# One VectorE operation for mask, negation, copy and row minimum in the attention of a hybrid decoder kernel

## The chip, the cores and the metric

The kernel runs on one core of one Trainium2 chip. Its engines work side by side and are tied by semaphores: TensorE (PE) for matmuls, with its weight loads (PEld), VectorE (DVE), ScalarE (ACT), GpSimd (POOL) and SyncE (SP), which here only issues transfers. The metric is the device time of one execution in microseconds (us), the median of several runs.

## The reference

Everything is float32, with 1024 positions of width 1024. One RG-LRU layer comes first, then one attention layer of 8 heads, whose keys and values are projected from the stream after the first layer, and a last norm. The attention works on blocks of 128 queries, and a causal mask leaves a query the keys up to its own place:

```
def one_block(args):                     # one block of 128 queries
    qn_b, qr_b, bi = args
    s = einsum("bqhd,bkhd->bhqk", qn_b, k_nope) + einsum("bqhr,bkr->bhqk", qr_b, k_rope)
    s = s * ATTN_SCALE
    mask = kpos[None, :] <= (bi * 128 + arange(128))[:, None]
    p = softmax(where(mask, s, -inf), axis=-1)
    return einsum("bhqk,bkhd->bqhd", p, v)
...
o = lax.map(one_block, ...)              # 8 blocks x 8 heads
y = o * silu(gate);  x = x + y @ w_out;  return rms_norm(x, final_norm)
```

## The kernel before

Each float32 operand of a matmul is split in a high half and a low half, and a product is the sum of three matmuls. The high half is an ACT copy (L82), the low half a DVE subtraction that follows it (L83).

The attention runs from about 528 to 785 us, some 31 us a head. For each head `kq` projects keys and queries (matmuls at L114 to L116), `vals` the values of two heads (L839 to L841). Query block number qb sees nk = 128(qb+1) keys, so the eight blocks of a head have 128, 256, ... 1024 columns. In the text a block goes by its columns ("block 1024"). `scores` does, for one block:

- five matmuls on each stretch of up to 512 columns (L857 to L861) into a tile `s` of PSUM, of which there are two;
- L862, DVE: the triangular 128x128 mask is added to the last 128 columns, in PSUM;
- L864, DVE: the negated maximum of each row, over the whole block, into `m`;
- L867, ACT: exp(s + m) from PSUM into a page of SBUF, with the row sum `l`; a second instruction reads the sum out (ACTIVATION_READ_ACCUMULATOR in the trace). Its end gives the tile `s` back;
- L868 and L869, DVE: one over `l`, and the page times it.

Then `transposes` turns the page by TensorE in squares of 128 (L877) into PSUM tiles `pm`, and L82 and L83 split them into `pt`. After every fourth block `pv` multiplies values by `pt` (L892 to L894), and L896 multiplies by the gate. Scores are issued two blocks ahead (LOOK = 2).

In the last head the output projection is prepared too: `wout` loads a slice of its weights (L920 by SP into `wr`, of which there are two; L922 by POOL) and makes its low half on DVE (L923), and `dpart` runs first parts of that projection on TensorE while blocks are waited for. 36 pages of 128x1024 in SBUF are shared by all of this.

The order of the instructions on each engine is fixed at build time by a scheduler that follows priorities. At run time each engine goes through its list in order and waits where an operand or a buffer is not ready.

Of the kernel before, what the change touches and what calls it, by code (L numbers as in the profile page):

```python
# [9 lines left out]
F32 = mybir.dt.float32  # L10
F32R = mybir.dt.float32r
AF = mybir.ActivationFunctionType
ALU = mybir.AluOpType
AX = mybir.AxisListType
# [3 lines left out]
S = 1024  # L18
# [6 lines left out]
NEG = -1e30  # L25
P = 128
# [31 lines left out]
def trunk(tc, xT, wina, vecs, wgate, wouta, winc, wuk, wuv, wuq, wuqr, woutb, rope, outT):  # L58
    nc = tc.nc
    V, A, T, G = nc.vector, nc.scalar, nc.tensor, nc.gpsimd  # L60
# [10 lines left out]
    def nm(s):  # L71
        uid[0] += 1
        return f"{s}_{uid[0]}"

    def page(dt=F32R):
        return pgs.tile([P, S], dt, tag="pg", name=nm("pg"))
# [89 lines left out]
    mask = con.tile([P, P], F32, name="mask")  # L166
# [636 lines left out]
    tp = pt.enter_context(tc.tile_pool(name="tp", bufs=2, reuse_waits="tile"))  # L803

    vt = {}

    def kq(hd):

        wk, wq = wtile(wuk[hd], 2), wtile(wuq[hd], 3)
        k, q = (page(), page()), (page(), page())  # L810
        qs = tp.tile([P, S], F32R, tag="qs", name=nm("qs"))
        for c in range(4):
            nc.sync.dma_start(out=f(qs[32 * c:32 * c + 32, :]), in_=qsd[c, 32 * hd:32 * hd + 32, :])

        def proj(w, src, dst, h):
            ps = pm()
            mmt(ps, w, src, hs(h))
            hl(ps, dst[0][:, hs(h)], dst[1][:, hs(h)])

        work = [lambda a=a, h=h: proj(*a, h) for a in ((wq, cq, q), (wk, ckv, k)) for h in range(2)]  # L820
        return (k, q, qs), work
# [24 lines left out]
    def scores(hd, qb, k, q, qs):  # L846
        nk = (qb + 1) * P
        ps = pss.tile([P, S], F32, tag="s", name=nm("s"))
        ql = slice(qb * P, nk)

        o = P if nk == 5 * P else 0
        sc = ps[:, o:o + nk]
        for c0, c1 in ((0, min(nk, HW - o)), (HW - o, nk)):
            if c0 >= c1:
                continue
            c = slice(c0, c1)
            T.matmul(out=sc[:, c], lhsT=q[0][:, ql], rhs=k[0][:, c], start=True, stop=False)  # L857
            T.matmul(out=sc[:, c], lhsT=q[0][:, ql], rhs=k[1][:, c], start=False, stop=False)  # L858
            T.matmul(out=sc[:, c], lhsT=q[1][:, ql], rhs=k[0][:, c], start=False, stop=False)  # L859
            T.matmul(out=sc[:, c], lhsT=qs[:, ql], rhs=R1[:, c], start=False, stop=False)  # L860
            T.matmul(out=sc[:, c], lhsT=qs[:, ql], rhs=R2[:, c], start=False, stop=True)  # L861
        V.tensor_tensor(out=sc[:, ql], in0=sc[:, ql], in1=mask, op=ALU.add)  # L862
        m = tp.tile([P, 1], F32, tag="m", bufs=4, name=nm("m"))
        V.tensor_reduce(out=m, in_=sc, axis=AX.X, op=ALU.max, negate=True)  # L864
        p_ = page(F32)
        l = tp.tile([P, 1], F32, tag="l", bufs=4, name=nm("l"))
        A.activation(out=p_[:, 0:nk], in_=sc, func=AF.Exp, bias=m, accum_out=l)  # L867
        V.reciprocal(out=l, in_=l)  # L868
        V.tensor_scalar(out=p_[:, 0:nk], in0=p_[:, 0:nk], scalar1=l, scalar2=None, op0=ALU.mult)  # L869
        return p_  # L870
# [75 lines left out]
    for i in range(LOOK):  # L946
        pend[items[i]] = scores(*items[i], *heads[0])
    for i, (hd, qb) in enumerate(items):
# [8 lines left out]
        if i + LOOK < len(items):  # L957
            nh = items[i + LOOK]
            if nh[1] == 0 and nh[0]:
                while kqwork:  # L960
                    kqwork.pop(0)()
            pend[nh] = scores(*nh, *heads[nh[0]])
# [151 lines left out]
```

## Time and profile before

| | us |
|---|---|
| median of 3 runs | 876.18 (875.81 to 876.95) |
| profiled execution | 876.11 |
| its span in the trace | 874.3 |
| PE busy | 857.5 (98%) |
| DVE busy | 659.4 (75%) |
| ACT busy | 517.0 (59%) |
| POOL busy | 75.1 (9%) |
| mean granted TensorE clock | 0.994 of full speed |

The span is cut out of the profiled execution by the trace; 1.8 us lie around it. A timeline row gives the start and the length of one instruction (or of several alike, with their count), and in brackets how long the engine stood idle before it and which instruction released it. Instructions of an engine overlap a little in the records: the next one starts some 0.08 us before the one ahead has ended, so a row's start to the next row's start is what an instruction takes from its engine.

### The profile page before, as it was taken

Reading aid. Unit: us, or ns where it says so; the run is one execution under the profiler, and the core shown is the slowest. Engines: PE = TensorE matmul, PEld = TensorE weight load, DVE = VectorE, ACT = ScalarE, POOL = GpSimd, SP = SyncE. Lnnn points to the kernel's source line nnn. Section 1 sums busy time; section 2 is a strip of 40 time slices with the busy share of each in tenths; the row PEclk is TensorE's granted clock in tenths of the full one; section 3 lists DMA queues with packets and bytes.
Section 4 is the critical chain, followed back from the end, with each engine's and each line's share of the span. In section 5 each row is a group of like instructions: output and inputs, shape, how many; then the busy total and the mean of one; then the engine's idle time right before and its main releaser. Section 6 shows DMA issues by size and latency. Waiting matters only on the chain.

```text
span 874.3 us, 12183 instructions
## 1 busy us (share of the span) xinstructions
PE 857.5 (98%) x4326; PEld 729.6 (83%) x4326; DVE 659.4 (75%) x1224; ACT 517.0 (59%) x956; POOL 75.1 (9%) x145
## 2 busy tenths in 40 slices
PE   8999999999999999999999999999999999999995
PEld 7788888888887888888778888988998998888995
DVE  7798778777877764779988956887797887775453
ACT  7457787777687542699885645555565554431222
POOL 1010110011000100000212320000000000010000
PEclk9999999999999999999999999999999999999998
DMA  8333333333212545133535664222231326666031
GB/s 289 99 97 97 97 96 97 109 101 92 79 37 81 179 132 175 49 108 111 177 122 205 216 229 119 76 82 97 70 112 67 111 67 258 214 216 204 27 126 66
DMA packets 51789, 109.00 MB, mean 125 GB/s; under 512 B 6544, under 2 KB 16656, under 8 KB 51728
## 3 DMA queue, kind: packets, MB, share of 16 engines
q1 hardware_dynamic: 36240, 67.45, 24.2%
q0 software_dynamic: 15216, 40.51, 13.9%
q8 instruction: 34, 0.56, 0.3%
q10 hardware_dynamic: 272, 0.26, 0.1%
q14 instruction: 27, 0.22, 0.1%
HBM read 81.46 MB, written 26.21 MB: 123 GB/s over the span
## 4 chain that ended last, share of the span: by engine, by line
PE 62%; issue 21%; DVE 7%; ACT 4%; DMA 2%; POOL 2%; SPq 0%; DVEq 0%; POOLq 0%; ACTq 0%
PE ps L115 7%; PE ps L116 7%; PE ps L114 7%; PE pm L116 6%; PE pm L115 6%; PE pm L114 6%; PE pm L877 4%; PE pm L894 2%; PE pm L893 2%; PE s L858 2%; PE s L859 2%; PE s L857 2%; PE s L861 2%; PE s L860 2%; PE pm L892 2%
## 5 line engine op out<-in xcount | busy, mean ns | idle before, releaser
L114 PE MATMUL ps<-pg,wh 128*128 128x512 f32 x672 | 262.4, 392 | 3.4 <-DVE tk L627 1.2
L115 PE MATMUL ps<-pg,wh 128*128 128x512 f32 x672 | 262.4, 390 | 0.3 <-DVE pg L262 0.3
L116 PE MATMUL ps<-pg,wl 128*128 128x512 f32 x672 | 262.2, 390 | 0.1
L114 PEld LDWEIGHTS ps<-pg,wh 128*128 128x128 f32 x672 | 126.4, 188 | 31.9 <-DVE tk L627 1.6
L115 PEld LDWEIGHTS ps<-pg,wh 128*128 128x128 f32 x672 | 126.5, 188 | 27.7 <-DVE pg L262 0.6
L116 PEld LDWEIGHTS ps<-pg,wl 128*128 128x128 f32 x672 | 126.6, 188 | 27.1 <-DVE wl L83 1.0
L82 ACT ACTIVATE pt<-pm 128x512 fp32r<-128x512 f32 (+2 forms) x96 | 44.4, 490 | 59.0 <-PE pm L877 55.8
L867 ACT ACTIVATE pg<-s,m 128x128 f32<-128x128 f32 (+3 forms) x64 | 47.5, 743 | 48.0 <-DVE m L864 43.3
L114 PE MATMUL pm<-pg,pg 128*128 128x256 f32 (+1 forms) x192 | 61.9, 322 | 0.0
L115 PE MATMUL pm<-pg,pg 128*128 128x256 f32 (+1 forms) x192 | 61.6, 321 | 0.0
L116 PE MATMUL pm<-pg,pg 128*128 128x256 f32 (+1 forms) x192 | 61.3, 319 | 0.0
L83 DVE TENSOR_TENSOR pt<-pm,pt 128x512 fp32r<-128x512 f32 (+2 forms) x96 | 50.6, 547 | 2.2 <-ACT pt L82 2.1
L864 DVE TENSOR_REDUCE m<-s 128x1 f32<-128x128 f32 (+3 forms) x64 | 48.1, 753 | 1.0
L83 DVE TENSOR_TENSOR wl<-wr,wh 128x512 fp32r<-128x512 f32 (+2 forms) x57 | 32.8, 578 | 17.2 <-ACT wh L82 17.1
L358 DVE SCALAR_TENSOR_TENSOR t<-xb,vec,t 128x512 f32<-128x512 f32 x60 | 44.8, 746 | 0.4
L82 ACT ACTIVATE wh<-wr 128x512 fp32r<-128x512 f32 (+2 forms) x57 | 30.8, 543 | 23.8 <-PE ps L115 9.7
L82 ACT ACTIVATE pg<-pg 128x512 fp32r<-128x512 f32 x42 | 26.2, 630 | 29.9 <-DVE pg L412 18.3
L877 PE MATMUL pm<-ident,pg 128*128 128x128 f32 x288 | 42.3, 274 | 0.3 <-DVE pg L869 0.3
L116 PE MATMUL pm<-pg,wl 128*128 128x512 f32 x108 | 42.3, 392 | 0.0
L115 PE MATMUL pm<-pg,wh 128*128 128x512 f32 x108 | 42.3, 392 | 0.0
L114 PE MATMUL pm<-pg,wh 128*128 128x512 f32 x108 | 42.1, 390 | 0.0
L857 PE MATMUL s<-pg,pg 128*128 128x512 f32 (+2 forms) x96 | 37.2, 388 | 2.0 <-ACT pg L867 2.0
(223 smaller groups left out, 1789.6 us busy)
## 6 DMA issues: line engine op xcount, KB each, us to landing
wr<-wina SPq DMA_DIRECT2D x40, 256.0 KB, 2.8
wh<-wina POOLq DMA_DIRECT2D x36, 256.0 KB, 2.9
wa<-winc SPq DMA_DIRECT2D x24, 256.0 KB, 2.7
ysd<-pg POOLq DMA_DIRECT2D x12, 512.0 KB, 3.2
pg<-ysd SPq DMA_DIRECT2D x12, 512.0 KB, 8.3
wr<-wouta SPq DMA_DIRECT2D x16, 256.0 KB, 2.7
t<-xT SPq DMA_DIRECT2D x16, 256.0 KB, 4.0
x1d<-t POOLq DMA_DIRECT2D x16, 256.0 KB, 3.4
```

What stands on the lines that cost most here:

```text
L82: A.activation(out=hi, in_=src, func=AF.Copy)
L83: V.tensor_tensor(out=lo, in0=src, in1=f(hi), op=ALU.subtract)
L114: T.matmul(out=ps, lhsT=w[0], rhs=r[0], start=first, stop=False, skip_group_check=more)
L115: T.matmul(out=ps, lhsT=w[0], rhs=r[1], start=False, stop=False, skip_group_check=more)
L116: T.matmul(out=ps, lhsT=w[1], rhs=r[0], start=False, stop=last, skip_group_check=more)
L358: V.scalar_tensor_tensor(out=xc, in0=xb[:, j:j + HW], scalar=cwv[j], in1=xc, op0=ALU.mult, op1=ALU.add)
L857: T.matmul(out=sc[:, c], lhsT=q[0][:, ql], rhs=k[0][:, c], start=True, stop=False)
L858: T.matmul(out=sc[:, c], lhsT=q[0][:, ql], rhs=k[1][:, c], start=False, stop=False)
L859: T.matmul(out=sc[:, c], lhsT=q[1][:, ql], rhs=k[0][:, c], start=False, stop=False)
L864: V.tensor_reduce(out=m, in_=sc, axis=AX.X, op=ALU.max, negate=True)
L867: A.activation(out=p_[:, 0:nk], in_=sc, func=AF.Exp, bias=m, accum_out=l)
L877: T.transpose(out=ps[:, (b - b0) * P:(b - b0 + 1) * P], in_=p_[:, b * P:(b + 1) * P], identity=ident)
```

## The change

A page `maskw` is made once: 896 zero columns and then the 128 columns of the mask. Its last nk columns are the mask of a whole block. One DVE operation then reads the scores from PSUM and `maskw` from SBUF, writes -(s + mask) to the SBUF page and gathers the least of each row in `m` (which is the negated maximum). The exponential reads that page and writes it in place, with scale -1. In the changed kernel the lines from there on have numbers higher by 3: the new operation is L868, the exponential L870, the reciprocal L871, the scaling L872, the transposes L880, the products with the values L895 to L897, the gate L899 and the low half of `wout` L926.

```
+    maskw = page(F32)
+    G.memset(maskw[:, 0:S - P], 0.0)
+    G.tensor_copy(out=maskw[:, S - P:], in_=mask)
...
-        V.tensor_tensor(out=sc[:, ql], in0=sc[:, ql], in1=mask, op=ALU.add)
         m = tp.tile([P, 1], F32, tag="m", bufs=4, name=nm("m"))
-        V.tensor_reduce(out=m, in_=sc, axis=AX.X, op=ALU.max, negate=True)
         p_ = page(F32)
+        V.tensor_tensor_reduce(out=p_[:, 0:nk], in0=sc, in1=maskw[:, S - nk:], scale=-1.0, scalar=-NEG, op0=ALU.add, op1=ALU.min, accum_out=m)
         l = tp.tile([P, 1], F32, tag="l", bufs=4, name=nm("l"))
-        A.activation(out=p_[:, 0:nk], in_=sc, func=AF.Exp, bias=m, accum_out=l)
+        A.activation(out=p_[:, 0:nk], in_=p_[:, 0:nk], func=AF.Exp, scale=-1.0, bias=m, accum_out=l)
```

The new operation is two instructions on DVE: the main one, and one that writes `m` (128x1). Where each engine's list stands at two places follows. First DVE at the first blocks of the first head, before (`s` are the score tiles, `m` the row values, `l` the sums, `pg` pages):

```order
L862 TENSOR_TENSOR s_4849<-s_4849,mask 128x128
L862 TENSOR_TENSOR s_4863<-s_4863,mask 128x128
L864 TENSOR_REDUCE m_4856<-s_4849 128x1
L864 TENSOR_REDUCE m_4870<-s_4863 128x1
L868 RECIPROCAL l_4859<-l_4859 128x1
L869 TENSOR_SCALAR pg_4858<-pg_4858,l_4859 128x128
```

and now (the page read last is `maskw`):

```order
L868 ISA pg_4859,m_4858<-s_4852,pg_4769 128x128
L868 ISA m_4858 128x1
L868 ISA pg_4872,m_4871<-s_4865,pg_4769 128x256
L868 ISA m_4871 128x1
L868 ISA pg_4908,m_4907<-s_4901,pg_4769 128x384
L868 ISA m_4907 128x1
L871 RECIPROCAL l_4861<-l_4861 128x1
L872 TENSOR_SCALAR pg_4859<-pg_4859,l_4861 128x128
```

The operation of the third block has moved ahead of the first block's scaling. On PE the transpose of block 128 has moved behind the scores of the fourth block there.

The second place is DVE at the end of the last head, from the gate of block 512 on. Before, the mask additions and maxima of blocks 768 and 896 stood ahead of this piece, and it reads:

```order
L896 TENSOR_TENSOR pg_7405<-pm_7613,pg_7405 128x512
L923 TENSOR_TENSOR pg_7549<-wr_7550,pg_7548 128x512
L923 TENSOR_TENSOR pg_7549<-wr_7554,pg_7548 128x512
L868 RECIPROCAL l_7572<-l_7572 128x1
L869 TENSOR_SCALAR pg_7571<-pg_7571,l_7572 128x768
L868 RECIPROCAL l_7601<-l_7601 128x1
L869 TENSOR_SCALAR pg_7600<-pg_7600,l_7601 128x896
L83 TENSOR_TENSOR pg_7628<-pg_7405,pg_7627 128x512
L83 TENSOR_TENSOR pt_7610<-pm_7631,pt_7609 128x4x128
L83 TENSOR_TENSOR pt_7612<-pm_7638,pt_7611 128x128
L862 TENSOR_TENSOR s_7642<-s_7642,mask 128x128
L864 TENSOR_REDUCE m_7654<-s_7642 128x1
```

Now it begins with:

```order
L899 TENSOR_TENSOR pg_7350<-pm_7553,pg_7350 128x512
L83 TENSOR_TENSOR pt_7550<-pm_7571,pt_7549 128x4x128
L926 TENSOR_TENSOR pg_7491<-wr_7492,pg_7490 128x512
L926 TENSOR_TENSOR pg_7491<-wr_7496,pg_7490 128x512
L868 ISA pg_7511,m_7510<-s_7499,pg_4769 128x768
L868 ISA m_7510 128x1
L868 ISA pg_7539,m_7538<-s_7527,pg_4769 128x896
L868 ISA m_7538 128x1
L83 TENSOR_TENSOR pg_7568<-pg_7350,pg_7567 128x512
L871 RECIPROCAL l_7513<-l_7513 128x1
L83 TENSOR_TENSOR pt_7552<-pm_7578,pt_7551 128x128
L872 TENSOR_SCALAR pg_7511<-pg_7511,l_7513 128x768
```

The work on the scores of blocks 768 and 896 has moved behind the gate and a pair of weight subtractions. Some rows on, the next pair of weight subtractions, which stood side by side before the last two low halves of `pt`, now stands one by one among the low halves of blocks 896 and 1024, and its second one is just ahead of the low half that the last `pv` needs first. Over the middle of the attention the list of PE is the same as before; on POOL the filling of `maskw` (a memset and a copy) stands behind the last load of the key and value inputs, ahead of the last stores of the gates.

## Rows read from the trace of the kernel before

**Rows 1.** Windows: stretch, length, busy time (count) by engine, clock, DMA, GB/s

```profile
540.00:740.00 200.00, 200.00 (x1204) 179.48 (x1203) 163.87 (x362) 109.89 (x246) 6.93 (x13) 1.00 0.30 99
```

**Rows 2.** Waits of PE, 530 to 780: what for, us in all, times, longest

```profile
PE s L857 <- ACT pg L867: 2.0, 2, 1.1
PE pm L877 <- DVE pg L869: 0.3, 1, 0.3
```

**Rows 3.** Timeline of PE, first head: start, length, instruction, [idle before <- releaser]

```profile
532.55 0.28 PE L861 MATMUL s<-pg,qs 128*128 128x256 f32 x1
533.91 0.44 PE L857 MATMUL s<-pg,pg 128*128 128x384 f32 x1 [1.07 <-ACT pg L867]
```

**Rows 4.** Timeline of DVE, same place

```profile
532.66 0.51 DVE L862 TENSOR_TENSOR s<-s,mask 128x128 f32<-128x128 f32 x2 [3.15 <-PE s L861]
```

**Rows 5.** Groups of DVE by shape, whole span: busy us, mean ns, idle before

```profile
L358 DVE SCALAR_TENSOR_TENSOR t<-xb,vec,t 128x512 f32<-128x512 f32 x60 | 44.8, 746 | 0.4
L83 DVE TENSOR_TENSOR pt<-pm,pt 128x512 fp32r<-128x512 f32 x48 | 32.5, 680 | 0.7 <-ACT pt L82 0.6
...
L409 DVE TENSOR_TENSOR_SCAN t<-t,t,t 128x512 f32<-128x512 f32 x10 | 12.8, 1278 | 0.0
...
L864 DVE TENSOR_REDUCE m<-s 128x1 f32<-128x1024 f32 x8 | 9.8, 1224 | 0.3
```

**Rows 6.** Groups of ACT by shape, 528 to 790

```profile
L82 ACT ACTIVATE pg<-pm 128x512 fp32r<-128x512 f32 x45 | 25.8, 593 | 3.5 <-PE pm L841 3.4
L867 ACT ACTIVATION_READ_ACCUMULATOR pg<-s,m 128x1 f32 x64 | 12.4, 194 | 0.0
L82 ACT ACTIVATE pg<-pg 128x512 fp32r<-128x512 f32 x16 | 10.1, 631 | 11.2 <-DVE pg L896 10.8
L867 ACT ACTIVATE pg<-s,m 128x1024 f32<-128x1024 f32 x8 | 8.9, 1117 | 2.0 <-DVE m L864 2.0
```

**Rows 7.** Timeline of POOL, between the key and value loads and the gates' stores

```profile
518.48 1.15 POOL L777 DMA_DIRECT2D gd<-tk  x2 [10.59 <-ACT tk L776]
```

**Rows 8.** Groups of POOL, whole span

```profile
L1058 POOL TENSOR_TENSOR pg<-pg,acc 128x256 f32<-128x256 f32 x2 | 1.8, 898 | 88.9 <-DVE acc L151 88.9
```

**Rows 9.** Timeline of DVE, end of the second head

```profile
594.61 0.68 DVE L83 TENSOR_TENSOR pt<-pm,pt 128x512 fp32r<-128x512 f32 x1
```

**Rows 10.** Timeline of PE, same place

```profile
596.82 0.39 PE L893 MATMUL pm<-pt,pg 128*128 128x512 f32 x1
```

**Rows 11.** Timeline of DVE, block 1024 of the seventh head

```profile
742.45 0.30 DVE L862 TENSOR_TENSOR s<-s,mask 128x128 f32<-128x128 f32 x1 [0.17 <-PE s L861]
```

**Rows 12.** Timeline of PE, start of the last head

```profile
745.30 0.39 PE L857 MATMUL s<-pg,pg 128*128 128x256 f32 x1 [0.94 <-ACT pg L867]
...
746.44 1.06 PE L877 MATMUL pm<-ident,pg 128*128 128x128 f32 x8 [0.28 <-DVE pg L869]
```

**Rows 13.** Timeline of DVE, second half of the last head

```profile
760.72 0.96 DVE L864 TENSOR_REDUCE m<-s 128x1 f32<-128x768 f32 x1
...
765.85 1.09 DVE L864 TENSOR_REDUCE m<-s 128x1 f32<-128x896 f32 x1
766.92 0.69 DVE L896 TENSOR_TENSOR pg<-pm,pg 128x512 f32<-128x512 f32 x1
...
771.65 0.29 DVE L862 TENSOR_TENSOR s<-s,mask 128x128 f32<-128x128 f32 x1
...
773.23 1.02 DVE L83 TENSOR_TENSOR pt<-pm,pt 128x512 fp32r<-128x512 f32 x2
774.60 0.16 DVE L868 RECIPROCAL l<-l 128x1 f32<-128x1 f32 x1 [0.35 <-ACT pg L867]
...
778.00 1.28 DVE L83 TENSOR_TENSOR pt<-pm,pt 128x512 fp32r<-128x512 f32 x2
781.13 0.69 DVE L923 TENSOR_TENSOR pg<-wr,pg 128x512 fp32r<-128x512 f32 x1 [1.85 <-DMA wr<-woutb]
```

**Rows 14.** Timeline of PE, the last pv

```profile
778.74 0.50 PE L892 MATMUL pm<-pt,pg 128*128 128x512 f32 x1
```

## The prediction

> **What bounds the kernel now.** I read the busy times of the page first (the table above): PE is at 98% of the span. Then the window over the middle of the attention: in the 200 us from 540 on PE is busy for all 200 at full clock, DVE for 163.87, ACT for 109.89, POOL for 6.93 [rows 1]. So over most of the stretch that the change touches, an instruction taken from DVE or ACT gives nothing by itself, as long as what PE reads next is ready in time. What can be gained stands in the waits of PE: three in the whole attention, 2.0 us for the exponential to give back a score tile and 0.3 us for a scaled page [rows 2]. The timelines put them at two places: 1.07 us at 533.91, where the third block of the first head wants the first block's tile [rows 3], and 0.94 and 0.28 us at 745.30 and 746.44, around block 1024 of the seventh head [rows 12]. 2.29 us is all that PE idles there. What can be lost stands at the end of the last head, where the last `pv` starts at 778.74 [rows 14], while the DVE operation that makes its first low half, the first of two from 778.00 (1.28 us for both, some 0.68 for one), ends at 778.68 [rows 13]: PE goes on as soon as DVE delivers.
>
> **The change part by part.** Removed per block: a mask addition of 0.29 us [rows 13] and a maximum, 1.22 us at 1024 columns [rows 5]. Added: one operation over the block and a read of its accumulator.
>
> The new operation isn't in the trace. From below, nothing in it can go faster than one column per cycle with two sources, as the low-half subtraction does: 680 ns at 512 columns, and the maximum at 1024 continues that line (1224, that is 1.06 ns per further column; at 128 columns it gives 0.27 us) [rows 5]. From above, the scan (L409) takes 1278 ns at 512 [rows 5], 0.60 more than the subtraction, or 1.17 ns more per column. I take the lower end: the scan carries each column's result into the next, where the new operation adds two sources and only gathers a minimum. The accumulator read lies between about 0.07 us (what a 128x1 operation costs its engine when it overlaps its neighbour; 0.16 long in [rows 13]) and the 0.19 us of ACT's own such read [rows 6]; I take 0.1. So a block costs 0.29 - 0.1, some 0.2 us less on DVE: 64 blocks, 12 us of DVE time. It lies beside a PE that is busy throughout, so its worth is nothing but for the two places. If the cover of 36 us of idle DVE in 200 were gone, the same 12 us would count.
>
> The exponential reads SBUF instead of PSUM. A copy of 512 columns takes 631 ns from SBUF and 593 from PSUM [rows 6]: 0.04 us a block, 2.4 in all on an engine with 90 idle us in 200 [rows 1]; where it stands in a chain that PE waits for I count it in the roundings. From below it is nothing.
>
> POOL fills `maskw` before the gates' last stores. A POOL operation over 256 columns took 898 ns [rows 8], so 1024 columns are at most 3.6 us, and POOL is idle for 10.59 us there [rows 7]: nothing. The page held leaves 35 for the rest; PE's list in the middle is unchanged, so I cost it at nothing; at the worst a load of the last head starts later, which is in the third rival.
>
> First place (first head). The new operation on block 128 starts where the mask addition did, 532.66 [rows 4], and ends at 532.93, with its read at about 533.05. That gives the tile back; before, the exponential did. PE was ready at 533.91 - 1.07 = 532.84 [rows 3], so it starts at about 533.05 to 533.1: -0.8 us. What is late next would be the transpose of block 128, since the new operation of the third block now stands ahead of the scaling. That operation ends at about 534.9, the scaling some 0.6 later at 535.5; PE has moved the transpose behind the next scores (five matmuls of 0.23 and two more), to about 535.8. Nothing.
>
> Second place (seventh to last head). The operation on block 1024 starts at 742.45 [rows 11] and ends, with its read, at 743.75. The tile is then free before PE wants it (745.30 - 0.94 = 744.36 [rows 12]), so the 0.94 goes. But the transposes of block 1024 at 746.44 then want the scaled page 0.94 + 0.28 earlier, at 745.22. The exponential, 1.12 us at 1024 columns [rows 6], from 743.8 to 744.95, its sum's reading and the reciprocal, some 0.3, and the scaling of some 0.75 put it at 746.05. The wait moves there: 746.44 becomes 746.05, -0.4 us.
>
> The middle. The first low half of the last blocks of the second head starts at 594.61, ends at 595.29 [rows 9], and the matmul that reads it starts at 596.82 [rows 10]: 1.5 us to spare. Where addition and maximum were apart with other work between them, the whole operation now comes first, which can put that work off by what the maximum took beyond a mask addition, 0.9 us at most (1224 against 290). That is under 1.5: nothing.
>
> Third place (end of the last head). DVE's list decides. Before, the maxima of blocks 768 and 896 ran at 760.72 and 765.85, in time where DVE otherwise waited. From the gate at 766.92 to the low half at 778.00 are 11.08 us [rows 13]. Now these two stand behind the gate: +0.96 and +1.09, less two overlaps of 0.08, with two reads of 0.1: +2.1. On block 1024, from 771.65 to 773.23, 1.58 becomes 1.23 - 0.08 + 0.1 = 1.25: -0.33. The wait of 0.35 at 774.60 [rows 13] goes, since DVE is now the late one. Weight subtractions are as many in this stretch as before. Sum +1.4, and up to 0.6 more where the subtraction just behind the gate must wait for ACT's half of block 640; I put in half of it, +0.3. A short stall comes ahead of it: the operation on block 512 now stands behind two low halves of 256 and 384 columns (0.4 and 0.5 us by the slope above), and its tile is wanted soon after; I put in 0.2, with 0 and 0.9 as ends. What follows the last `pv` has no slack to give back: PE is full to the end.
>
> Sum, from the profiled execution's 876.11: -0.8 - 0.4 + 0.2 + 1.4 + 0.3 = +0.7, so 876.8. That execution lies 0.07 below the median of the runs, which I leave out.
>
> [...]
>
> **The rivals.** 1: the waits of PE go and nothing comes in their place, as DVE makes up for the moved work at the end of the last head. 876.11 - 1.07 - 0.94 - 0.28 = 873.8. For it speaks that DVE has 12 us less to do; against it, that instructions run in the order of the list, and that the last low half is on time by 0.06 us now. With a chain that grows by half of what I put in, 876.8 - 0.85 gives 875.95, which is the forecast's own case still. Chance 0.17.
>
> 2, on the slower side: two cycles per column. At the end three operations with 768 + 896 + 1024 = 2688 columns stand in the chain: +3.1. At the second place block 1024 takes 1.2 more: +1.2. In the middle 1.2 more stays within the 1.5 to spare. 876.8 + 4.3 = 881.1. For it speaks the scan's row; against it the maximum and the subtractions, all at one column per cycle. It decides from about 0.4 ns per column on. Chance 0.12.
>
> 3, slower: the weight subtraction that now stands just ahead of the last low half waits for its load, and holds that half with it. Its load can only start when the pair before it, which is now behind the gate's next low half, has given back `wr`. The next subtraction waited 1.85 us for such a load [rows 13]. With 1.85 and the other half of the wait for ACT, 876.8 + 1.85 + 0.3 = 878.95, some 879. Against it: before, the pair ran just ahead of 778.00 [rows 13] with no wait. It decides once the load lands after about 777. Chance 0.16.
>
> **How the numbers follow.** The forecast has 0.55, with 875.6 to 878.0 as its own range (a chain grown by half and no wait for ACT; or that wait and the stall at block 512 in full, and an accumulator read of 0.19 on each of the three blocks). A measurement of this kernel can tell 0.2%, 1.75 us, from no change. Faster by that needs 874.4: the first rival in full, some 0.14 with the forecast's tail. Slower by that needs 877.9: the second and third, 0.28, and 0.05 of the forecast's tail. The rest, 0.53, is the same. The range 874.2 to 880.6 leaves out most of the second rival and part of the first.
>
> **What would show it.** In the changed profile: no wait at the third block's scores of the first head beyond 0.3 us; PE waiting for the scaling of block 1024 at the seventh head's end, not for a tile; the new operation at about 0.69 us for 512 columns and 1.23 for 1024, with a short instruction behind it; DVE's busy time some 12 us lower; and a PE wait of 1 to 2 us at or ahead of the last `pv`, for a low half or a scaled page. Operations near 1.3 us at 512 columns, waits of PE between 560 and 740, or a wait for a load in the last head would make the prediction wrong; so would no wait at the last `pv`.

## The result: 1.4 us slower, less than the 0.2% that could be told beforehand

22 runs of each kernel, side by side, gave 877.26 us against 875.88, a ratio of 1.0015 with a 95% interval of 1.0009 to 1.0021. A second set, with 11 runs of the changed kernel, gave 876.61 against 875.88, 1.0011 (1.0002 to 1.0019). The forecast was 876.8. The profiled execution of the changed kernel took 876.46 us, its span 874.7.

The busy times of the page, over the whole span (engine, busy us, share, instructions):

```profile
PE 857.6 (98%) x4326; PEld 729.4 (83%) x4326; DVE 648.7 (74%) x1224; ACT 518.4 (59%) x956; POOL 76.3 (9%) x147
```

DVE has 10.7 us less to do than the 659.4 of before; I had put in 12. ACT has 1.4 more. The window over the middle of the attention, which answers to [rows 1] (columns as there):

```profile
540.00:740.00 200.00, 200.00 (x1203) 179.44 (x1203) 155.87 (x362) 112.11 (x249) 6.93 (x13) 1.00 0.31 101
```

PE is still busy for all 200 us: 8 us of DVE work taken away there moved nothing. The waits of PE in the attention (what for, us in total, times, longest), for [rows 2]:

```profile
PE pm L895 <- DVE pt L83: 0.9, 1, 0.9
PE pm L880 <- DVE pg L872: 0.6, 1, 0.6
PE pm L880 <- DVE pt L83: 0.5, 1, 0.5
PE s L860 <- DVE m L868: 0.2, 1, 0.2
```

No wait for the exponential to give back a tile is left, and two waits for low halves have come. With the hundredths of the rows below they are 0.21, 0.60, 0.54 and 0.95, 2.30 us in all against the 2.29 of before. The new operation in the groups of DVE by shape, and the exponential in those of ACT (busy us, mean ns, idle before), for [rows 5] and [rows 6]:

```profile
L868 DVE CUSTOM_DVE_ANT_0 pg<-s,pg 128x1024 f32<-128x1024 f32 x8 | 9.8, 1224 | 1.4 <-PE s L864 1.2
...
L868 DVE CUSTOM_DVE_ANT_0 pg<-s,pg 128x512 f32<-128x512 f32 x8 | 5.5, 688 | 2.4 <-PE s L864 2.4
...
L868 DVE DVE_READ_ACCUMULATOR2_ANT m<- 128x1 f32 x64 | 5.2, 82 | 0.0
...
L868 DVE CUSTOM_DVE_ANT_0 pg<-s,pg 128x128 f32<-128x128 f32 x8 | 2.2, 281 | 3.2 <-PE s L864 3.2
```

```profile
L870 ACT ACTIVATE pg<-pg,m 128x1024 f32<-128x1024 f32 x8 | 9.2, 1154 | 0.0
```

The operation takes what the maximum alone took, 1224 ns at 1024 columns and 688 at 512; the accumulator read takes 82 ns. The exponential takes 37 ns more than the 1117 of before. The places, on PE's timeline (start, length, instruction, wait and releaser), for [rows 3], [rows 12] and [rows 14]:

```profile
527.57 0.22 PE L860 MATMUL s<-pg,pg 128*128 128x128 f32 x1
...
532.80 0.44 PE L860 MATMUL s<-pg,pg 128*128 128x384 f32 x1 [0.21 <-DVE m L868]
```

```profile
744.06 0.34 PE L861 MATMUL s<-pg,pg 128*128 128x384 f32 x1
744.99 1.06 PE L880 MATMUL pm<-ident,pg 128*128 128x128 f32 x8 [0.60 <-DVE pg L872]
```

```profile
776.74 1.12 PE L880 MATMUL pm<-ident,pg 128*128 128x128 f32 x8 [0.54 <-DVE pt L83]
778.80 0.50 PE L895 MATMUL pm<-pt,pg 128*128 128x512 f32 x1 [0.95 <-DVE pt L83]
```

And DVE at the end of the last head, for [rows 13]:

```profile
765.21 0.69 DVE L899 TENSOR_TENSOR pg<-pm,pg 128x512 f32<-128x512 f32 x1 [1.55 <-PE pm L897]
766.36 0.69 DVE L83 TENSOR_TENSOR pt<-pm,pt 128x512 fp32r<-128x512 f32 x1 [0.46 <-ACT pt L82]
766.97 1.28 DVE L926 TENSOR_TENSOR pg<-wr,pg 128x512 fp32r<-128x512 f32 x2
768.17 0.95 DVE L868 CUSTOM_DVE_ANT_0 pg<-s,pg 128x768 f32<-128x768 f32 x1
...
769.05 1.08 DVE L868 CUSTOM_DVE_ANT_0 pg<-s,pg 128x896 f32<-128x896 f32 x1
...
771.80 1.23 DVE L868 CUSTOM_DVE_ANT_0 pg<-s,pg 128x1024 f32<-128x1024 f32 x1 [0.20 <-PE s L864]
...
774.69 0.75 DVE L872 TENSOR_SCALAR pg<-pg,l 128x1024 f32<-128x1024 f32 x1
775.39 0.69 DVE L926 TENSOR_TENSOR pg<-wr,pg 128x512 fp32r<-128x512 f32 x1
...
777.06 0.68 DVE L926 TENSOR_TENSOR pg<-wr,pg 128x512 fp32r<-128x512 f32 x1
778.06 1.29 DVE L83 TENSOR_TENSOR pt<-pm,pt 128x512 fp32r<-128x512 f32 x2 [0.32 <-ACT pt L82]
```

The operations on blocks 768 and 896 stand behind the gate and the weight subtractions, DVE is late from there on, and the low half for the last `pv` starts only at 778.06, after a weight subtraction and a wait of 0.32 for ACT. That is as late as before (778.00), though PE was by then some 1.8 us further on than before the change: 0.23 on entering the attention, and 0.86 and 0.69 at the two places (worked out below). From the gate to this low half are 12.85 us now (765.21 to 778.06), against the 11.08 of before: +1.77.

To compare executions that enter the attention at different times I take the time from the first score matmul to the start of the last instruction of PE in the trace (two matmuls that end the last norm). Before it runs from 527.80 to 864.64, 336.84 us; now from 527.57 to 864.69, 337.12: **+0.28**. In a second profile of the changed kernel it is 337.19, +0.35. That is the change's own share up to there; the text below calls it the stretch.

Behind it stands one more difference, which the prediction doesn't have. From the start of that last instruction to the end of the span are 9.67 us before, and 10.00 and 10.01 in the two profiles of the changed kernel, since the last transfers of the output take longer from issue to landing (tiles, engine, count, KB, median us; before, then the changed kernel):

```profile
outT<-pg SPq DMA_DIRECT2D x3, 256.0 KB, 2.5
outT<-pg ACTq DMA_DIRECT2D x1, 256.0 KB, 2.4
```

```profile
outT<-pg SPq DMA_DIRECT2D x3, 256.0 KB, 3.0
outT<-pg ACTq DMA_DIRECT2D x1, 256.0 KB, 3.0
```

With these 0.33 us the change costs +0.61 and +0.68 in the two profiles. Why the transfers take longer is open.

### The profile page after: what moved, and what is told of

Its sections match the earlier page's. It is cut to its first block, busy times and chain, and to the rows that moved or that the text cites. A ratio compares the mean times of both kernels' runs of the same rounds, so it can differ in the third digit from the quotient of the medians.

```text
span 874.7 us, 12173 instructions
## 1 busy us (share of the span) xinstructions
PE 857.6 (98%) x4326; PEld 729.4 (83%) x4326; DVE 648.7 (74%) x1224; ACT 518.4 (59%) x956; POOL 76.3 (9%) x147
## 4 chain that ended last, share of the span: by engine, by line
PE 75%; issue 11%; DVE 7%; ACT 4%; DMA 2%; POOL 1%; DVEq 0%; SPq 0%; POOLq 0%; ACTq 0%
PE ps L115 12%; PE ps L114 12%; PE ps L116 12%; PE pm L115 6%; PE pm L116 6%; PE pm L114 6%; PE pm L880 3%; PE s L861 2%; PE s L862 2%; PE pm L896 2%; PE pm L897 2%; PE s L860 2%; PE s L863 2%; PE s L864 2%; PE pm L895 2%
## 5 line engine op out<-in xcount | busy, mean ns | idle before, releaser
L870 ACT ACTIVATE pg<-pg,m 128x128 f32<-128x128 f32 (+3 forms) x64 | 49.6, 775 | 24.2 <-DVE m L868 23.4
L868 DVE CUSTOM_DVE_ANT_0 pg<-s,pg 128x128 f32<-128x128 f32 (+3 forms) x64 | 47.9, 751 | 8.4 <-PE s L864 8.0
L880 PE MATMUL pm<-ident,pg 128*128 128x128 f32 x288 | 42.3, 274 | 1.1 <-DVE pg L872 0.6
L82 ACT ACTIVATE pg<-pm 128x512 fp32r<-128x512 f32 x48 | 28.2, 587 | 22.3 <-PE pm L116 14.3
```

The lines of the kernel that those rows point to most:

```text
L82: A.activation(out=hi, in_=src, func=AF.Copy)
L868: V.tensor_tensor_reduce(out=p_[:, 0:nk], in0=sc, in1=maskw[:, S - nk:], scale=-1.0, scalar=-NEG, op0=ALU.add, op1=ALU.min, accum_out=m)
L870: A.activation(out=p_[:, 0:nk], in_=p_[:, 0:nk], func=AF.Exp, scale=-1.0, bias=m, accum_out=l)
L880: T.transpose(out=ps[:, (b - b0) * P:(b - b0 + 1) * P], in_=p_[:, b * P:(b + 1) * P], identity=ident)
```

## The experiments

My theory: the tiles that come back early gain 1.5 us, the operations that have moved behind the gate in the last head lose 1.8, and nothing else of the change reaches PE. The rival: the operation, or the page, costs something in each head.

**The changed kernel again.** No edit.

> The changed kernel once more, for a second profile and the spread of its runs. Theory 1 (the end of the last head is late because the operations on blocks 768 and 896 moved behind the gate; the score tiles come back earlier): the attention in its profile shows again about 0.2 us of wait at the third block of the first head, 0.6 at block 1024 of the seventh, and together about 1.5 at and ahead of the last pv, in all some 0.3 us longer than before. Theory 2 (the new operation costs in every head, by itself or by the page that it needs): waits of PE in the middle heads in at least one more profile, 0.2 us or more each. Both expect 877.3 us by the runs so far.

Measured 876.61 us (before 875.88). The waits are the same four, to 0.03 us, and there is none in the middle heads. So the pattern is fixed; the second theory has nothing to show in the middle.

**The new operation in seven heads, and in the eighth alone.** The first of the two:

```
+        if hd < NH - 1:                  # the other kernel: hd == NH - 1
             V.tensor_tensor_reduce(out=p_[:, 0:nk], in0=sc, in1=maskw[:, S - nk:], ...)
             A.activation(out=p_[:, 0:nk], in_=p_[:, 0:nk], func=AF.Exp, scale=-1.0, ...)
+        else:
+            V.tensor_tensor(out=sc[:, ql], in0=sc[:, ql], in1=mask, op=ALU.add)
+            V.tensor_reduce(out=m, in_=sc, axis=AX.X, op=ALU.max, negate=True)
+            A.activation(out=p_[:, 0:nk], in_=sc, func=AF.Exp, bias=m, accum_out=l)
```

> The new operation in heads 1 to 7 only; the eighth head has the mask addition and the maximum again (maskw stays till the end of the seventh head). The DVE list of the eighth head is then that of the kernel before. Theory 1: the gains of the first head (0.85) and of the seventh (0.5 or more) stay and the loss at the last pv goes: 874.4 us, 1.5 less than before. Theory 2: seven eighths of the loss stay: 877 or more.

> The other half: the new operation in the eighth head only. Theory 1: the waits of the first and seventh head as before, and 1.5 us of new wait at and ahead of the last pv: 877.5 us. Theory 2: an eighth of the loss, 876.0.

Measured 875.09 (ratio 0.9986, 0.9977 to 0.9994) and 877.42 (1.0018, 1.0009 to 1.0026). The waits of PE in the attention, seven heads first, then the eighth alone:

```profile
PE pm L885 <- DVE pg L877: 1.2, 1, 1.2
PE s L860 <- DVE m L870: 0.2, 1, 0.2
```

```profile
PE s L860 <- ACT pg L875: 2.0, 2, 1.1
PE pm L900 <- DVE pt L83: 0.9, 1, 0.9
PE pm L885 <- DVE pt L83: 0.5, 1, 0.5
```

The change falls apart into a gain and a loss: the stretch is 1.15 us shorter with seven heads and 1.47 longer with the eighth alone, +0.32 together, where both at once gave +0.28 and +0.35. The second theory, which shares the loss out over the heads, falls. With seven heads the gain is 0.35 smaller in the stretch than I expected. The scaling of block 1024 is no later there (it starts 216.56 us after the first score matmul, in the changed kernel 216.52), and the transposes of that block start no later either. But PE's list puts these transposes straight behind the five score matmuls of block 256, as before the change, where the changed kernel runs two more score matmuls first; so PE waits 1.2 us instead of 0.6:

```profile
742.57 0.28 PE L864 MATMUL s<-pg,qs 128*128 128x256 f32 x1
744.05 1.06 PE L885 MATMUL pm<-ident,pg 128*128 128x128 f32 x8 [1.19 <-DVE pg L877]
```

**Fused, but not moved to SBUF.** The operation writes in place to PSUM.

```
-        V.tensor_tensor_reduce(out=p_[:, 0:nk], in0=sc, ...)
+        V.tensor_tensor_reduce(out=sc, in0=sc, ...)
-        A.activation(out=p_[:, 0:nk], in_=p_[:, 0:nk], func=AF.Exp, scale=-1.0, ...)
+        A.activation(out=p_[:, 0:nk], in_=sc, func=AF.Exp, scale=-1.0, ...)
```

> Fused, but not moved: the one operation writes the negated scores back to PSUM in place, and the exponential reads them there, as before, and gives the tile back. The operation needs no page, and on DVE's list it stands for blocks 768 and 896 ahead of the gate, as the maxima did. Theory 1: no new wait at the last pv; the tile comes back at the exponential's end, but that starts earlier (the operation is 0.2 us shorter than the pair, and two blocks don't interleave): -0.6 at the first head, -0.3 at the seventh, 875.0 us. Theory 2 by the operation itself: 877 or more; theory 2 by the page that it needs: 875 too.

Measured 875.68 (0.9998, 0.9989 to 1.0007), 0.7 above what I expected and the same as before within its interval; the stretch is 0.49 shorter. One kind of wait is left, and its two places:

```profile
PE s L860 <- ACT pg L870: 1.4, 2, 0.8
```

The fusion by itself costs nothing and gains little: the tile comes back when the exponential ends, 0.3 us earlier at each place, where I had expected 0.6 at the first. The rest of the gain is the move to SBUF. The loss is gone too, and it was the move that brought it: an operation that writes to a page stands elsewhere on DVE's list than one that doesn't.

**Two operations in place.** To pin that down, only those of blocks 768 and 896 of the last head write to PSUM, the other 62 to a page.

```
+        moved = hd < NH - 1 or qb not in (5, 6)
+        if moved: ...                    # as in the changed kernel
+        else: ...                        # in place, as just above
```

> The changed kernel, but for two operations: those of blocks 768 and 896 of the eighth head write in place to PSUM and need no page (their exponentials read PSUM). On DVE's list both then stand ahead of the gate, the one of block 640 stays among the weight subtractions, and the pair of weight subtractions between the last low halves is together again. Theory 1 (these two operations are the whole loss): no wait at the last pv, waits of 0.2 and 0.6 at the two places ahead of it, 1.5 us less than the kernel before in the attention, 874.6 us as with six blocks in place. Theory 2 (block 640, or the eighth head's operations taken together): part of the 1.5 us of wait at the last pv stays, 875.3 or more.

Measured 875.0 against 876.1 (0.9988, 0.9978 to 0.9998). The waits of PE, and DVE at the end of the last head:

```profile
PE pm L887 <- DVE pg L879: 0.6, 1, 0.6
PE s L860 <- DVE m L870: 0.2, 1, 0.2
```

```profile
761.30 0.96 DVE L874 CUSTOM_DVE_ANT_0 s<-s,pg 128x768 f32<-128x768 f32 x1
...
763.21 1.10 DVE L874 CUSTOM_DVE_ANT_0 s<-s,pg 128x896 f32<-128x896 f32 x1 [0.29 <-PE s L864]
...
764.23 0.69 DVE L906 TENSOR_TENSOR pg<-pm,pg 128x512 f32<-128x512 f32 x1
...
775.15 1.28 DVE L83 TENSOR_TENSOR pt<-pm,pt 128x512 fp32r<-128x512 f32 x2
```

No wait is left at the last `pv`; the operations run at 761.30 and 763.21, ahead of the gate at 764.23, and the last low halves start at 775.15, 2.91 us earlier than in the changed kernel; 1.11 of that is an earlier start of the attention. The stretch is 1.34 us shorter than before, and so 1.62 shorter than the changed kernel's: those two operations are nearly all of the loss. The time is 0.4 above what I expected. The pair of weight subtractions came back together with the two operations, so this run alone doesn't tell the two apart; the run with the weights one block later tells more.

**In place in six blocks of the last head.** `moved = hd < NH - 1 or qb < 2`, else as above.

> The fused operation everywhere, written to a page in heads 1 to 7 and in the first two blocks of the eighth, and in place to PSUM in the other six blocks of the eighth. Theory 1 (what costs is only that blocks 768 and 896 of the eighth head stand behind the gate; what gains is that tiles come back early at the first head and at block 1024 of the seventh): waits of 0.2 at the first head and 0.6 at block 1024, none at the last pv. Against the kernel before -0.85 and -0.65 in the attention, 1.5 in all, and 0.3 better than with the old pair in the eighth head: 874.4 to 874.8 us. Theory 2 (the old pair in the eighth head was what helped): no better than 875.1.

Measured 874.55 us against 875.87, 0.9984 (0.9976 to 0.9993): the best of these kernels, faster than both. Its waits are the two that are expected, and its stretch is 1.66 us shorter:

```profile
PE pm L887 <- DVE pg L879: 0.6, 1, 0.6
PE s L860 <- DVE m L870: 0.2, 1, 0.2
```

**The weights one block later.** `WOUT_AT = (-1, 2, 3)` in place of `(-1, 1, 2)`.

> The changed kernel with two of the three weight slices of the last head prepared one block later. On DVE's list block 768 then stands ahead of the gate again, and block 896 still behind it. Theory 1: half of the moved work is back in its place, so the wait at and ahead of the last pv falls from 1.5 to about 0.5 us: 876.0 to 876.4 us. Theory 2 (not the order of blocks 768 and 896 but the weight subtraction between the last low halves sets it, which stays there): as the changed kernel.

Measured 875.5 (0.9992, 0.9983 to 1.0001), below the 876.0 to 876.4 that I expected. The stretch is 0.60 shorter than before, so 0.9 of the loss has gone with the operation on block 768 back in its place; a wait of 0.74 stays at the last `pv`. The weight subtraction between the last low halves, which stayed, isn't enough to explain the loss; in the kernel with all operations in place one stands there too, at 775.11, and no wait follows. What the later weights alone do to the kernel before was not run.

**The page held, nothing fused.** The kernel before, which also makes `maskw` and takes the mask from its last 128 columns.

> The kernel before, which also fills maskw, holds its page through the attention and reads the mask from it; nothing is fused. Theory 1: DVE's list is that of before, and a page less costs nothing: same as before, 875.9. Theory 2 (a page less makes loads of the last head late): up to 1 us more, with a wait for a load in the last head.

Measured 876.03 (1.0001, 0.9992 to 1.001), a stretch of 336.83 against 336.84, with the three waits of before. A page less costs nothing by itself.

**The operation twice in five heads.** It is done twice for every block of the second to sixth head.

```
-        V.tensor_tensor_reduce(...)
+        for _ in range(2 if 1 <= hd <= 5 else 1):
+            V.tensor_tensor_reduce(...)
```

> The changed kernel, with the new operation done twice in a row for each block of the second to sixth head (same operands, same result): the price of a slow operation in the middle. It adds 8 operations a head, 6.0 us to the 24.4 that DVE is busy of 31. Theory A (my prediction's: the 1.5 us to spare at the last pv of a head take what block 1024 adds, about 1.2): no wait in the middle, as the changed kernel, 877. Theory B (what the other blocks add counts too, DVE has 30.3 of 31 us to do and its list makes PE wait): waits in each of the five heads, 1 to 2 us a head, 882 to 887.

Measured 879.28 (1.0036, 1.0023 to 1.0048), 2.0 to 2.7 above the changed kernel; the stretch is 339.84 us, 2.7 longer. One of the five heads in a window (columns as above), and the waits that are new or longer:

```profile
591.00:622.00 31.00, 30.81 (x185) 27.18 (x185) 28.30 (x73) 17.08 (x39) 1.07 (x2) 1.00 0.26 87
```

```profile
PE pm L881 <- DVE pg L83: 1.1, 5, 0.4
PE pm L881 <- DVE pt L83: 1.0, 1, 1.0
```

Neither theory has it. DVE goes from 24.4 to 28.3 us of 31, not to 30.3, since parts of instructions overlap (the lengths of the instructions that start in this window add up to 6.3 us more than in the changed kernel, the busy time to 4 more). PE waits 0.2 to 0.4 us in each of the five heads, and its matmuls fall 2.2 us back between the first head and the seventh, 0.45 a head. What of this stands in no wait goes with PE's list, which here isn't that of the changed kernel either: the transposes of block 1024 are split in two groups. The other 0.5 us is in the last head, where the wait of 0.54 is now 1.02. So 30 us of operations added to DVE in the middle cost 2.2, some 7% of their time, while taking 8 us in 200 away gave nothing.

## Why the prediction was right, step by step

The measured 877.26 lies in the range, on the forecast's side of 875.88 and inside the 0.2%. By the steps:

- **The operation** was taken at the maximum's time, 0.1 us for its read: 1224 ns and 82 ns measured. The second rival, which took the scan's 1.17 ns more per column, is out: from 688 ns at 512 columns to 1224 at 1024 the operation takes 1.05 ns per further column, and the prediction had read 1.06 from the subtraction and the maximum. Its "one column per cycle" is its name for that slope, and that nothing with two sources goes faster was my estimate from those rows: the traces don't show the cycle of DVE.
- **The first place**, -0.8: the wait went from 1.07 to 0.21, -0.86.
- **The second place**, -0.4: the transposes of block 1024 moved from 746.44 to 744.99, where the changed kernel was 1.10 ahead already (0.23 when it came into the attention and 0.86 from the first head, rounded): -0.35. Another 0.34 came that I had not put in: PE's list puts two score matmuls of the next block ahead of those transposes (the one at 744.06 is the second), and they run while PE would wait (the kernel with the new operation in seven heads lacks them there, and lacks this gain). Together -0.69.
- **The middle**, 0: no wait. But the working there was weaker than its result. I took the 1.5 us to spare at one matmul for the slack of a head; with the operation done twice PE waited at the transposes of block 1024, another place, so the second rival's price lacked about 2 us.
- **The end of the last head**, +0.2 + 1.4 + 0.3 = +1.9: by the other terms and the stretch of +0.28 it is 0.28 + 0.86 + 0.69 = +1.83. The chain from the gate to the last low half, which I had at +1.4 + 0.3, grew by 1.77. The waits of PE in it are 0.54 and 0.95. The stall at block 512 (0.2) didn't come; the wait for ACT behind the gate did (0.46 at 766.36), and another 0.32 at 778.06. Some 0.3 us of the loss stand in no wait: PE's list of the last head interleaves scores and products differently, and that this costs the rest is argued, not shown.
- **The first rival**, nothing in place of the waits: those 0.54 and 0.95 came in their place. DVE did not make up for the moved work.
- **The third rival**, a late load ahead of the last low half: the weight subtraction at 777.06 waited for nothing.

Sum: +0.7 forecast, +0.28 and +0.35 in the two profiled stretches, +0.61 and +0.68 with the last transfers, +1.38 and +0.73 in the medians. The terms in the attention held to 0.4 us, with the second place as the one that was too small. What follows the last `pv` I had put at nothing, as PE is full to the end; but the last transfers start behind PE's end and took 0.33 more. These two errors cancel, so that the sum comes as near as +0.61 is partly luck. The medians of the other kernels agree with stretch and last transfers to 0.25 us (0.4 for the operation done twice, with 5 runs): from the start of PE's last instruction to the end are 9.67 or 9.68 us in the kernels with the eighth head alone, the later weights, the held page and the operation done twice, and some 10.0 in the other four. Of the first set's +1.38 some 0.7 is left open; the last section has what is known of it.

Not shown is why the scheduler puts an operation that writes to a page behind the gate. That the pages of the last head come free late would do it, and it fits that two operations without a page go back to their place; but the moment at which each page comes free isn't in these traces.

## What to carry to other kernels

Where one engine is busy throughout, merging two operations of another is worth what the waits of the first one lose (here 1.07 us became 0.21 and 1.22 became 0.60, while 8 us of DVE work taken out of 200 moved nothing), and that came more from giving a buffer back one stage earlier (with the merge in place in PSUM the first wait lost only 0.31 of its 1.07 us, with the move 0.86) than from the shorter work. A merged operation needs all its outputs at once: here it needs the page that only the exponential needed before, so it may be put later in the order, and its whole length with it (here 0.95 and 1.08 us, for blocks 768 and 896). Look at the drain of the pipeline (the last head, the last block) first; splitting the change by stage showed in two runs that it was a gain and a loss of the same size, and the kernel that keeps the one without the other is 0.16% faster than before.

## What the runs showed that I had not expected

The executions of one kernel come into the attention at different times. The first score matmul starts at 527.57 us in one profile of the changed kernel and at 529.02 in the other, and over all the kernels here, whose code ahead of it is all but the same, between 526.35 and 529.02. The first 20 us of the two profiles of the changed kernel, the one of the result first (columns as above, the clock before the last two):

```profile
0.00:20.00 20.00, 18.26 (x72) 15.16 (x73) 14.07 (x29) 15.55 (x19) 2.37 (x10) 1.00 0.87 308
```

```profile
0.00:20.00 20.00, 16.60 (x60) 13.09 (x61) 13.04 (x28) 14.51 (x18) 1.12 (x8) 0.83 0.85 296
```

The clock was granted in full in the first and at 0.83 in the second; from 20 to 40 us both have it in full. But the clock isn't all of it. The kernel with the page held has the full clock in these 20 us and comes in at 528.62:

```profile
0.00:20.00 20.00, 17.04 (x68) 13.25 (x69) 13.03 (x28) 14.51 (x18) 1.99 (x10) 1.00 0.86 297
```

What the late ones share is the last column. Of the four profiles that come in before 527.00 three moved 307, 311 and 313 GB/s in their first 20 us (for the fourth, with two operations in place, the figure isn't listed), the five after 527.75 moved 296 to 301; the two in between have 301 and 308. That slower loads at the start make an execution late fits this, and is not shown.

Of the changed kernel's 33 runs 17 have a mean clock of at least 0.996 (9 of the 22 in the first set, 8 of the 11 in the second), with a median of 876.38; of 74 runs of the kernel before for which it is listed, 61 have, with a median of 875.82. At that clock the change costs 0.56 us, which is near the +0.61 and +0.68 of the profiles. Whether the changed kernel starts at less than the full clock more often than the kernel before, or did so by chance in the first set, for which the clock of the kernel before isn't listed, stays open.

The read of the accumulator took 82 ns behind an operation that writes to SBUF and 142 ns behind one that writes to PSUM:

```profile
L867 DVE DVE_READ_ACCUMULATOR2_ANT m<- 128x1 f32 x64 | 9.1, 142 | 0.0
```
